# One input's load moved to another queue, and the result stored by one engine: a bilinear form on one core

## The chip, the core and the metric

The kernel runs on one core of one Trainium2 chip. A core has five engines, each with its own queue of instructions: TensorE (PE, the matrix products), VectorE (DVE), ScalarE (ACT), GpSimd (POOL) and SyncE (SP). Data move between the chip's main memory (HBM) and the on-chip memory (SBUF) by sixteen transfer engines, which every engine's DMA instructions feed: the profile calls the queue that GpSimd feeds q0 (software), that of SyncE q1 and that of ScalarE q10 (both hardware). TensorE's results are collected in a separate memory (PSUM) of eight banks.

The metric is the device time of one execution in microseconds. Several executions are timed, and the median counts.

## What is computed

```python
batch, dim_i, dim_j, dim_k = 32, 256, 256, 128
x: [32, 256]   y: [32, 256]   weight: [128, 256, 256]      (all float32)
out = np.einsum('bi,bj,kij->bk', x, y, weight)             # [32, 128]
```

For each of the 128 values of k the weight is a 256 x 256 matrix, and each row b of the result needs x[b] times that matrix times y[b]. The weight has 33.6 MB and is read once; x, y and the result have 32, 32 and 16 KB.

## The kernel before

**Tiling.** k is written as kk * 32 + g, with kk from 0 to 3 and g (a "group") from 0 to 31. The 128 partitions of the weight in SBUF hold four values of kk times 32 slices of i (ip), and each slice has eight values of i (ic). A group is thus a tile of 128 partitions x (8 x 256) values, 1 MB in float32. One product takes the weight of one or two groups at one ic (128 x 256 or 128 x 512) as the moving operand, and as the stationary one xblk[:, ic], a 128 x 128 matrix that holds x in four diagonal blocks, so that the four kk in the partitions stay apart. Eight products, one per ic, add up in PSUM. What comes out, for each group, is a tile of 128 (b, kk) x 256 (j). VectorE multiplies it by y4 (y repeated for each kk) and sums over j, which gives one column of acc [128 x 32].

**Order of the weight.** Thirty of the 32 groups are loaded by GpSimd (L120), which converts them to bfloat16 on the way, in eleven transfers listed in `LOADS`: of 2, 4, 8, 8, 4, 2 and 1 groups, and the last group in four pieces of 4, 2, 1 and 1 values of ic. Groups 0 and 16 (`FIRST`) are loaded as float32 into w_f, one by SyncE and one by ScalarE (L134), and ScalarE converts them (L178). TensorE goes through `UNITS`: 16 groups at once (all eight banks), then 8, 4, 2, 1 and 1. The first unit needs the two groups of `FIRST` and the first three of GpSimd's transfers, each of the later ones its own transfer or transfers. Since the first unit fills all banks, the second waits until VectorE's first product (L294) has freed them.

**The head.** All loads are issued ahead of the barrier with which the engines start (`hw` and `sw`, moved to the head of the program by hand). The queues then hold, in order:

- SyncE: w_f group 0
- ScalarE: x (L130), w_f group 16
- GpSimd: loads 1 and 2 of the weight, y (L127), loads 3 to 11

Behind the barrier GpSimd makes an identity matrix (L168, L169). VectorE's queue holds: the copy of x into x_rep (L192, waits for x), four transposes to xt (L198), the mask from the identity (L205), xblk in four instructions (L210); then y's transpose (L219, waits for y), its copy (L222) and four transposes to y4 (L227); then the products and sums of the units (L294, L298, and L302 for the two units of one group). TensorE's first product waits for w_f's conversion, for xblk and for the loads of its unit (L237).

**The tail.** When VectorE has written the last column of acc, ScalarE stores its partitions 64 to 127 (L311) and SyncE its partitions 0 to 63 (L313). Each then marks a semaphore; GpSimd waits for both marks, and resets the DMA queues' state and the semaphores (L315 to L317). SyncE's last instructions wait until both stores have landed and clear that semaphore (L318, L319).

Of the kernel before, what the change touches and what calls it, by code (L numbers as in the profile page):

```python
# [36 lines left out]
def kernel(  # L37
# [7 lines left out]
    nc = tc.nc  # L45
    P = 128
# [6 lines left out]
    B, I = x.shape  # L53
# [12 lines left out]
    def sbuf(name, shape, dtype):  # L66
        return nc.alloc_sbuf_tensor(name, shape, dtype).ap()

    def rows_of(groups):


        step = G // len(groups)
        assert all(g == groups[0] + n * step for n, g in enumerate(groups))
        v = weight.rearrange("(u s) (ip ic) j -> s ip u (ic j)", s=step, ic=IC)
        return v[groups[0]]

    def w_of(groups):
        at = [place_of[g] for g in groups]
        step = at[1] - at[0] if len(at) > 1 else 1
        assert all(a == at[0] + n * step for n, a in enumerate(at))  # L80
        return w_sb[:, at[0]:at[-1] + 1:step, :]
# [3 lines left out]
    x_sb = sbuf("x_sb", [B, I], f32)  # L85
    y_sb = sbuf("y_sb", [B, J], f32)
# [9 lines left out]
    acc = sbuf("acc", [P, G], f32)  # L96
# [6 lines left out]
        for s, (groups, lo, hi) in zip(s_w, LOADS) for g in groups for ic in range(lo, hi)  # L103
    }
    s_f = [nc.alloc_semaphore(f"f{g}") for g in FIRST]
    s_x = nc.alloc_semaphore("x")
    s_y = nc.alloc_semaphore("y")
# [3 lines left out]
    s_dve = nc.alloc_semaphore("dve")  # L111
    s_fin = nc.alloc_semaphore("fin")
    s_out = nc.alloc_semaphore("out")
# [5 lines left out]
    sw = [  # L119
        nc.gpsimd.dma_start(  # L120
            out=w_of(groups)[:, :, lo * J:hi * J],
            in_=rows_of(groups)[:, :, lo * J:hi * J],
        ).then_inc(s, 16).ins
        for (groups, lo, hi), s in zip(LOADS, s_w)
    ]

    sw.insert(2, nc.gpsimd.dma_start(out=y_sb, in_=y).then_inc(s_y, 16).ins)  # L127

    hw = [
        nc.scalar.dma_start(out=x_sb, in_=x).then_inc(s_x, 16).ins,  # L130
    ]
    for n, (g, queue) in enumerate(zip(FIRST, (nc.sync, nc.scalar))):
        hw.append(
            queue.dma_start(  # L134
                out=w_f[:, n:n + 1, :], in_=rows_of((g,)),
# [13 lines left out]
    for blk in blocks:  # L149
# [15 lines left out]
    pool, act, v, pe, sp = nc.gpsimd, nc.scalar, nc.vector, nc.tensor, nc.sync  # L165
# [4 lines left out]
        out=ident, in_=ident, compare_op=mybir.AluOpType.not_equal, fill=1.0,  # L170
# [13 lines left out]
    n_dve = 0  # L184

    def done(ins):
# [6 lines left out]
        out=x_rep,  # L193
        in_=x_sb.rearrange("b (ip ic) -> b ic ip", ic=IC).unsqueeze(3)
        .to_broadcast([B, IC, IP, KK]),
    )._wait_ge(s_x, 16))
    for q in range(Q):
        c = v.transpose(  # L198
            out=xt[q * 32:(q + 1) * 32, :, :],
            in_=x_rep[:, :, q * IP // Q:(q + 1) * IP // Q, :],  # L200
# [5 lines left out]
        out=mask, in_=ident.rearrange("p (ip kk) -> p kk ip", kk=KK), axis=AX, op=add,  # L206
    )._wait_ge(s_pool, 2))

    for kk in range(KK):
        c = v.tensor_scalar(  # L210
            out=xblk[:, :, :, kk], in0=xt, scalar1=mask[:, kk:kk + 1],
# [8 lines left out]
        out=yt, in_=y_sb.rearrange("b (jb j) -> b jb j", j=32),  # L220
    )._wait_ge(s_y, 16))
    t = done(v.tensor_copy(  # L222
        out=y_rep, in_=yt.unsqueeze(3).to_broadcast([B, J // 32, B, KK]),
    )._wait_ge(s_dve, t))
    BQ = B // Q
    for q in range(Q):
        c = v.transpose(  # L227
            out=y4[q * 32:(q + 1) * 32, :].rearrange("p (jb j) -> p jb j", j=32),
            in_=y_rep[:, :, q * BQ:(q + 1) * BQ, :],
# [22 lines left out]
    for u, unit in enumerate(UNITS):  # L252
# [40 lines left out]
        if n_g > 1:  # L293
            t = done(v.tensor_tensor(  # L294
                out=prod, in0=sums, in1=y4.unsqueeze(1).to_broadcast([P, n_g, J]), op=mult,
# [3 lines left out]
                out=acc[:, unit[0]:unit[-1] + 1:unit[1] - unit[0]], in_=prod, axis=AX, op=add,  # L299
            )._wait_ge(s_dve, t))  # L300
        else:
            done(v.tensor_tensor_reduce(  # L302
                out=prod[:, 0, :], in0=sums[:, 0, :], in1=y4, scale=1.0, scalar=0.0,
# [4 lines left out]


    out_v = out.rearrange("b (kk g) -> b kk g", kk=KK)  # L310
    act.dma_start(out=out_v[B // 2:], in_=acc[P // 2:, :])._wait_ge(s_dve, n_dve).then_inc(s_out, 16)  # L311
    act.sem_inc(s_fin, 1)
    sp.dma_start(out=out_v[:B // 2], in_=acc[:P // 2, :])._wait_ge(s_dve, n_dve).then_inc(s_out, 16)  # L313
    sp.sem_inc(s_fin, 1)
    pool.wait_ge(s_fin, 2)  # L315
    pool.dma_reset(range(nums[0], nums[-1] + 1))
    pool.sem_clear(range(nums[0], nums[-1] + 1))  # L317
    sp.wait_ge(s_out, 32)  # L318
    sp.sem_clear(s_out)  # L319


# [28 lines left out]
```

## Time and profile before

| | |
|---|---|
| time, median of 3 executions | 85.35 us (85.29 to 85.44) |
| profiled execution | 85.44 us, of which the span from the first to the last instruction is 84.1 us |
| busy in the span | PE 33.4 us, DVE 25.0, POOL 8.8, ACT 5.3, PEld 4.3 |
| DMA | 4928 packets; HBM read 33.62 MB |
| queue q0 (GpSimd) | 93.5% of the sixteen engines' span; q1 3.5%, q10 3.4% |
| TensorE's longest wait | 42.0 us, for the loads of w_sb |
| mean granted clock of TensorE | 0.959 |

The profile is that of one execution. PE is TensorE's products, PEld its loading of stationary operands, and an engine's name with a q is its sequencer, which issues DMAs. The strips cut the span into 40 slices of 2.1 us; each digit is a busy share in tenths. GB/s counts the bytes that were written, so a stream that converts float32 to bfloat16 shows half of what it reads. The chain is followed back from the last instruction, at each step to what released it; "another core or an unknown queue" is a releaser that the profile couldn't name, for which the list of waits gives the load. A timeline row gives start, duration, engine, line, operation and, in brackets, how long the engine had been idle and what released it; rows of several instructions give the stretch that they cover. Time to landing is from the start of an issue to the last completion mark.

### The profile page before, as it was taken

Reading aid. Unit: us, or ns where it says so; the run is one execution under the profiler, and the core shown is the slowest. Engines: PE = TensorE matmul, PEld = TensorE weight load, DVE = VectorE, ACT = ScalarE, POOL = GpSimd, SP = SyncE. Lnnn points to the kernel's source line nnn. Section 1 sums busy time; section 2 is a strip of 40 time slices with the busy share of each in tenths; the row PEclk is TensorE's granted clock in tenths of the full one; section 3 lists DMA queues with packets and bytes.
Section 4 is the critical chain, followed back from the end, with each engine's and each line's share of the span. In section 5 each row is a group of like instructions: output and inputs, shape, how many; then the busy total and the mean of one; then the engine's idle time right before and its main releaser. Section 6 shows DMA issues by size and latency. Waiting matters only on the chain.

```text
span 84.1 us, 259 instructions
## 1 busy us (share of the span) xinstructions
PE 33.4 (40%) x136; PEld 4.3 (5%) x43; DVE 25.0 (30%) x28; ACT 5.3 (6%) x5; POOL 8.8 (10%) x18
## 2 busy tenths in 40 slices
PE   0000000000000000000099999997009999997670
PEld 0000000000000000000000000000000010113320
DVE  0019540000291000000000000002999900799950
ACT  0019850000000000000000000000000000000000
POOL 5999500000000000000000000000000000000000
PEclk9999999999999999999999999999855599999999
DMA  4999999999999999999999999999999999999940
GB/s 121 390 362 288 216 216 216 216 214 216 214 216 216 218 216 214 216 210 214 210 218 216 216 216 214 216 216 208 214 214 216 216 216 214 216 208 212 197 59 8
DMA packets 4928, 17.91 MB, mean 213 GB/s; under 512 B 400, under 2 KB 816, under 8 KB 4672
## 3 DMA queue, kind: packets, MB, share of 16 engines
q0 software_dynamic: 4432, 15.76, 93.5%
q1 hardware_dynamic: 224, 1.06, 3.5%
q10 hardware_dynamic: 272, 1.09, 3.4%
HBM read 33.62 MB, written 0.02 MB: 400 GB/s over the span
## 4 chain that ended last, share of the span: by engine, by line
DMA 46%; PE 40%; DVE 6%; POOL 3%; another core or an unknown queue 2%; issue 1%; POOLq 0%
DMA w_sb<-in_weight_dram 46%; PE ps L237 40%; DVE tmp L294 5%; POOL w_sb L120 2%; POOL y_sb L127 1%; DVE tmp L302 1%; POOL const-float32-0.0 L334 0%; POOLq L334 0%; POOL const-uint8-127 L334 0%; POOL const-float32-1.0 L334 0%; DVE acc L302 0%
## 5 line engine op out<-in xcount | busy, mean ns | idle before, releaser
L237 PE MATMUL ps<-w_sb,xblk 128*128 128x512 bf16 (+1 forms) x136 | 33.4, 405 | 48.2 <-DMA w_sb<-in_weight_dram 43.5
L294 DVE TENSOR_TENSOR tmp<-ps,y 128x4096 f32<-128x4096 f32 (+3 forms) x4 | 8.6, 2151 | 37.6 <-PE ps L237 37.6
L298 DVE TENSOR_REDUCE acc<-tmp 128x16 f32<-128x4096 f32 (+3 forms) x4 | 8.6, 2154 | 0.1
L237 PEld LDWEIGHTS ps<-w_sb,xblk 128*128 128x128 bf16 x43 | 4.3, 101 | 77.1 <-DMA w_sb<-in_weight_dram 42.9
L120 POOL DMA_DIRECT2D w_sb<-in_weight_dram x11 | 7.6, 702 | 0.6 <-issue 0.6
L178 ACT CAST w_sb<-w_f 128x1024 bf16<-128x1024 f32 x4 | 4.0, 1042 | 0.3 <-DMA w_f<-in_weight_dram 0.3
L219 DVE STREAM_TRANSPOSE yt<-y_sb 32x256 f32<-32x256 f32 x1 | 0.4, 432 | 11.0 <-DMA y_sb<-in_y_dram 11.0
L192 DVE COPY x_rep<-x_sb 32x1024 f32<-32x1024 f32 x1 | 0.8, 790 | 6.1 <-PEq L334 6.1
L198 DVE STREAM_TRANSPOSE xt<-x_rep 32x256 f32<-32x256 f32 x4 | 1.7, 435 | 0.1
L227 DVE STREAM_TRANSPOSE y<-y_rep 32x256 f32<-32x256 f32 x4 | 1.7, 435 | 0.1
L178 ACT ACT_TABLE_LOAD x1 | 1.3, 1283 | 6.0 <-PEq L334 6.0
L210 DVE TENSOR_SCALAR xblk<-xt,mask 128x256 bf16<-128x256 f32 x4 | 1.4, 501 | 0.0
L302 DVE CUSTOM_DVE_ANT_0 tmp<-ps,y 128x256 f32<-128x256 f32 x2 | 0.8, 419 | 0.9 <-PE ps L237 0.9
L222 DVE COPY y_rep<-yt 32x1024 f32<-32x1024 f32 x1 | 0.7, 682 | 0.0
L205 DVE TENSOR_REDUCE mask<-ident 128x4 f32<-128x128 f32 x1 | 0.4, 380 | 1.0 <-POOL ident L169 1.0
L127 POOL DMA_DIRECT2D y_sb<-in_y_dram x1 | 0.5, 534 | 0.0
L169 POOL TENSOR_SCALAR_AFFINE_SELECT ident<-ident 128x128 f32<-128x128 f32 x1 | 0.3, 287 | 0.1
L168 POOL MEMSET ident<- 128x128 f32 x1 | 0.3, 289 | 0.0
L302 DVE DVE_READ_ACCUMULATOR2_ANT acc<- 128x1 f32 x2 | 0.2, 82 | 0.0
L334 POOL MEMSET const-float32-0.0<- 128x1 f32 x1 | 0.1, 98 | 0.2 <-issue 0.2
L334 POOL MEMSET const-bfloat16-1.0<- 128x1 bf16 x1 | 0.1, 101 | 0.0
L334 POOL MEMSET const-uint8-127<- 128x1 uint8 x1 | 0.1, 101 | 0.0
(1 smaller groups left out, 0.1 us busy)
## 6 DMA issues: line engine op xcount, KB each, us to landing
w_sb<-in_weight_dram POOLq DMA_DIRECT2D x2, 4096.0 KB, 48.1
w_sb<-in_weight_dram POOLq DMA_DIRECT2D x2, 2048.0 KB, 43.4
w_sb<-in_weight_dram POOLq DMA_DIRECT2D x2, 1024.0 KB, 41.0
w_f<-in_weight_dram SPq DMA_DIRECT2D x1, 1024.0 KB, 4.9
w_f<-in_weight_dram ACTq DMA_DIRECT2D x1, 1024.0 KB, 9.0
w_sb<-in_weight_dram POOLq DMA_DIRECT2D x1, 512.0 KB, 72.3
w_sb<-in_weight_dram POOLq DMA_DIRECT2D x1, 256.0 KB, 72.9
w_sb<-in_weight_dram POOLq DMA_DIRECT2D x1, 128.0 KB, 73.0
```

The source lines that it names most:

```text
L120: nc.gpsimd.dma_start(out=w_of(groups)[:, :, lo * J:hi * J], in_=rows_of(groups)[:, :, lo * J:hi * J],).then_inc(s, 16).ins
L127: sw.insert(2, nc.gpsimd.dma_start(out=y_sb, in_=y).then_inc(s_y, 16).ins)
L178: c = act.copy(out=w_sb[:, place_of[g], lo:hi], in_=w_f[:, n, lo:hi])
L192: t = done(v.tensor_copy(out=x_rep, in_=x_sb.rearrange("b (ip ic) -> b ic ip", ic=IC).unsqueeze(3) .to_broadcast([B, IC, IP, KK]),)._wait_ ...
L198: c = v.transpose(out=xt[q * 32:(q + 1) * 32, :, :], in_=x_rep[:, :, q * IP // Q:(q + 1) * IP // Q, :],)
L210: c = v.tensor_scalar(out=xblk[:, :, :, kk], in0=xt, scalar1=mask[:, kk:kk + 1], scalar2=None, op0=mult,)
L222: t = done(v.tensor_copy(out=y_rep, in_=yt.unsqueeze(3).to_broadcast([B, J // 32, B, KK]),)._wait_ge(s_dve, t))
L227: c = v.transpose(out=y4[q * 32:(q + 1) * 32, :].rearrange("p (jb j) -> p jb j", j=32), in_=y_rep[:, :, q * BQ:(q + 1) * BQ, :],)
L237: return pe.add_instruction(mybir.InstMatmult(name=nc.get_next_instruction_name(), engine=mybir.EngineType.PE, ins=[pe.lower_ap(rhs), pe.l ...
L294: t = done(v.tensor_tensor(out=prod, in0=sums, in1=y4.unsqueeze(1).to_broadcast([P, n_g, J]), op=mult,)._wait_ge(s_pe, n_pe))
L298: done(v.tensor_reduce(out=acc[:, unit[0]:unit[-1] + 1:unit[1] - unit[0]], in_=prod, axis=AX, op=add,)._wait_ge(s_dve, t))
L302: done(v.tensor_tensor_reduce(out=prod[:, 0, :], in0=sums[:, 0, :], in1=y4, scale=1.0, scalar=0.0, op0=mult, op1=add, accum_out=acc[:, uni ...
```

## The change

The load of x leaves the head of ScalarE's queue and becomes the third transfer in GpSimd's list, just ahead of y. At the end acc is stored by one transfer of 128 partitions, issued by SyncE, in place of two of 64; ScalarE stores nothing, and the marks that GpSimd and SyncE wait for are halved accordingly.

```diff
-    sw.insert(2, nc.gpsimd.dma_start(out=y_sb, in_=y).then_inc(s_y, 16).ins)
-
-    hw = [
-        nc.scalar.dma_start(out=x_sb, in_=x).then_inc(s_x, 16).ins,
+    sw[2:2] = [
+        nc.gpsimd.dma_start(out=x_sb, in_=x).then_inc(s_x, 16).ins,
+        nc.gpsimd.dma_start(out=y_sb, in_=y).then_inc(s_y, 16).ins,
     ]
+
+    hw = []
     for n, (g, queue) in enumerate(zip(FIRST, (nc.sync, nc.scalar))):
...
     out_v = out.rearrange("b (kk g) -> b kk g", kk=KK)
-    act.dma_start(out=out_v[B // 2:], in_=acc[P // 2:, :])._wait_ge(s_dve, n_dve).then_inc(s_out, 16)
-    act.sem_inc(s_fin, 1)
-    sp.dma_start(out=out_v[:B // 2], in_=acc[:P // 2, :])._wait_ge(s_dve, n_dve).then_inc(s_out, 16)
+    sp.dma_start(out=out_v, in_=acc)._wait_ge(s_dve, n_dve).then_inc(s_out, 16)
     sp.sem_inc(s_fin, 1)
-    pool.wait_ge(s_fin, 2)
+    pool.wait_ge(s_fin, 1)
     pool.dma_reset(range(nums[0], nums[-1] + 1))
     pool.sem_clear(range(nums[0], nums[-1] + 1))
-    sp.wait_ge(s_out, 32)
+    sp.wait_ge(s_out, 16)
     sp.sem_clear(s_out)
```

## The prediction

> **What bounds the kernel now.** I read the page's strips first, then the chain in order of time, then the timeline at the head and at the tail, then the DMA by small windows. The strips show one resource that is never idle between its start and its end:
>
> ```profile
> PE   0000000000000000000099999997009999997670
> ...
> DMA  4999999999999999999999999999999999999940
> GB/s 121 390 362 288 216 216 216 216 214 216 214 216 216 218 216 214 216 210 214 210 218 216 216 216 214 216 216 208 214 214 216 216 216 214 216 208 212 197 59 8
> ...
> HBM read 33.62 MB, written 0.02 MB: 400 GB/s over the span
> ```
>
> The transfer engines are full from the first slice to the 38th (a slice is 2.1 us). The 33.62 MB read between about 1.2 and 80.9 us are 0.42 MB per us. TensorE has half the span free. The chain at its end tells whether TensorE or the stream of weights ends last:
>
> ```profile
> 75.52 0.70 another core or an unknown queue
> ...
> 76.26 1.89 PE ps L237 x8
> 78.15 0.49 another core or an unknown queue
> ...
> 79.72 0.18 another core or an unknown queue
> ...
> 82.03 0.01 DVE acc L302
> ```
>
> Before each of the last small units TensorE waits (0.70, 0.49, 0.18 us); the waits' own view names the landing of w_sb. So the end follows the stream: whatever shifts its last packets shifts the last reduction by as much, and a delay of TensorE up to 0.7 us is swallowed. Behind the reduction stands only the store, both halves issued at 82.07, until the span closes at 84.1. Two places can therefore move the time: the length of the stream, and the 2.0 us of the store.
>
> **The change, part by part.** The profiled execution took 85.44 us: a span of 84.10 and 1.34 around it. It is the highest of the three (median 85.35); the terms are made against it and then laid on the median.
>
> ```profile
> 0.00 0.66 SPq L134 DMA_DIRECT2D w_f<-in_weight_dram  x1
> 0.12 0.43 ACTq L130 DMA_DIRECT2D x_sb<-in_x_dram  x1
> 0.59 0.62 ACTq L134 DMA_DIRECT2D w_f<-in_weight_dram  x1
> ...
> 2.65 0.53 POOL L127 DMA_DIRECT2D y_sb<-in_y_dram  x1
> 3.18 5.96 POOL L120 DMA_DIRECT2D w_sb<-in_weight_dram  x9
> ...
> 22.58 0.43 DVE L219 STREAM_TRANSPOSE yt<-y_sb 32x256 f32<-32x256 f32 x1 [11.04 <-DMA y_sb<-in_y_dram]
> ...
> 42.04 16.27 PE L237 MATMUL ps<-w_sb,xblk 128*128 128x512 bf16 x64 [42.04 <-DMA w_sb<-in_weight_dram]
> ```
>
> *x comes late, and it is hidden.* On GpSimd's queue x stands behind the same two loads as y, so it lands where y lands, near 22.5 us. VectorE's first instruction waits for x, and in its queue the mask, xblk and the whole of y's preparation stand behind it. From 22.5: the copy 0.79, four transposes 1.83, mask 0.38, xblk 1.37, together 4.4 us, so xblk is there at 27. Then y's own 0.43 + 0.68 + 1.83 = 2.9, so y4 is there at 30. TensorE's first product needs xblk and starts at 42.04 because of the third load; VectorE's first use of y4 is at 58.35. Cover 15 and 28 us: cost nothing. Without the cover each us would cost a us less the 0.7 of slack.
>
> *GpSimd issues one transfer more,* 0.53 us by y's row. The nine loads behind it go out 0.53 later, the first at 3.71 instead of 3.18; its turn on the transfer engines comes after y, near 22. Covered by 18 us. The identity matrix (9.07) and the start barrier, which waits for GpSimd and frees the other engines at about 6.0, move as much; the casts of w_f then end near 12.1 instead of 11.6, needed at 42.04. Nothing.
>
> *ScalarE loses x's issue* (0.43), so its w_f load is issued at about 0.12 instead of 0.59. That transfer is served after SyncE's w_f (landed at 4.9) and its data are not needed before 42: no gain of its own.
>
> *The stream gets x inside it.* Its 32 KB now stand in the saturated stretch: 0.033 MB / 0.42 = 0.08 us. The trace's packet records show y doing just this at 21.5 us: one packet per engine and a completion mark, 0.096 us until the next load's packets. I take +0.09, with 0.08 and 0.10 as ends.
>
> *The stream's start gets rid of x.* The windows at the head, then the two small waves of the store's halves (columns at the end: granted clock, DMA share, GB/s):
>
> ```profile
> 1.00:1.20 0.20, 0.00 (x0) 0.00 (x0) 0.00 (x0) 0.00 (x0) 0.15 (x1) 1.00 0.08 31
> 1.20:1.50 0.30, 0.00 (x0) 0.00 (x0) 0.00 (x0) 0.00 (x0) 0.30 (x1) 1.00 0.98 198
> 1.50:1.80 0.30, 0.00 (x0) 0.00 (x0) 0.00 (x0) 0.00 (x0) 0.30 (x1) 1.00 1.31 328
> ...
> 83.20:83.30 0.10, 0.00 (x0) 0.00 (x0) 0.00 (x0) 0.00 (x0) 0.00 (x0) 1.00 0.20 32
> ...
> 83.50:83.60 0.10, 0.00 (x0) 0.00 (x0) 0.00 (x0) 0.00 (x0) 0.00 (x0) 1.00 0.31 46
> ```
>
> By the packet records x runs from 1.17 to 1.53; w_f's first packets come at 1.43 to 1.71 on the sixteen engines, 1.54 in the mean. If x only held the engines up, w_f may start at its issue's end plus what x needed after its own: 0.66 + 0.63 = 1.29, a gain of 0.25 at most. If w_f's 128 rows simply take 1.43 us from issue to first packet, only the late engines gain, 0.05 to 0.1. It can also lose: the two w_f issues now stand side by side as the two halves of the store do, and there the one whose issue started 5 ns later got its packets 0.27 us after the other (83.24 and 83.51). SyncE's stays the first by 0.12 us, so I take -0.05, with -0.25 and +0.27 as ends.
>
> *The store in one piece.* SyncE's half landed 1.7 us after its issue, ScalarE's 2.0, and SyncE's wait for both ended the span.
>
> ```profile
> out_dram<-acc SPq DMA_DIRECT2D x1, 8.0 KB, 1.7
> out_dram<-acc ACTq DMA_DIRECT2D x1, 8.0 KB, 2.0
> ```
>
> No row shows a store of 128 rows. The times from the start of an issue to the first packet are 1.05 us for 32 rows (x), 1.18 for 64 (SyncE's half), 1.43 for 128 (w_f): 4 ns per row. So the single store's first packet would come at 82.07 + 1.43 = 83.50, just where the later half's came (83.51). Then each engine has eight packets instead of four, about 12 ns each by the records: +0.05. Ends: as quick as SyncE's half, 2.0 - 1.7 = -0.30; or the second half's packets spread out behind the first's for another 0.27 us on top of today's end, +0.27. I take +0.05, since three rows lie on one line. GpSimd's clean-up waits for one engine's mark instead of two; in the records it ends near 83.0, a microsecond before the span: nothing.
>
> A rule speaks to this part. The Trainium skill, page "DMA: Bandwidth & Descriptors", section "Rules for kernel authors", says that two transfers to disjoint partition halves serialize and that one 128-partition transfer is to be used; by it the merge costs nothing, the term would be 0 and the time 85.39. The two waves in the windows agree that the halves follow each other. The same page, "Latency and other measured facts", gives a first byte about 0.4 us later for a transfer issued from GpSimd than from ScalarE, which speaks against moving x; by it x would be late by 0.4 us, against the 20 us that the trace's y row shows.
>
> Sum: +0.09 - 0.05 + 0.05 = +0.09. On the profiled execution 85.53, on the median **85.44 us**.
>
> **The rivals.** A difference below 0.2% (0.17 us) can hardly be told from none here; the forecast lies below that.
>
> 1. *The store in one piece is the slower one.* Place: the last 2 us, where nothing overlaps. For it: x's 32 rows, two packets per engine, spread over 0.36 us, and w_f's first packets over 0.28, where a half of the store took 0.2. Price: +0.27 with +0.04 of the stream, 85.66. It decides once the store lands later than 2.13 us after its issue (0.13 + 0.04 = 0.17). Against it: the line of the three rows.
> 2. *The head of the stream is held up* by two 128-row issues side by side: +0.27 + 0.09 + 0.05, 85.76. For it: ScalarE's half of the store. Against it: x's issue lay inside that of w_f and delayed it by little or nothing.
> 3. *The store is as quick as SyncE's half:* -0.30 + 0.04, 85.09. It decides from a landing under 1.79 us. For it: one completion to wait for, and the wave of a half is gone. Against: twice the rows for one queue.
> 4. *x is late for TensorE.* It needs xblk after 42.0, so x after 37.6; y says 22.5. Should x's issue stall behind the third load (landing near 41), xblk would come near 46, and the end 4 - 0.7 = 3.3 us later, 88.7. Against: the order of the queue.
>
> **How the numbers follow.** Forecast (within 0.2%) 0.47; rival 1 0.21; rival 2 0.15; rival 3 0.15; rival 4 0.02. Slower is 0.21 + 0.15 + 0.02 = 0.38, faster 0.15. The range reaches from just above rival 3's price to rival 2's, 85.17 to 85.78: it leaves out most of rival 3, rival 4, and the far end of rival 2, some 2 in 10. The forecast's own range is 85.18 to 85.52.
>
> **What would show it.** In the profile after: x_rep starts near 22.6 and the first product near 42.1; the waits of TensorE before the last units are as long as before; the last products come 0.04 us later; one out store whose landing stands between 1.9 and 2.1. Wrong would be: a first product moved by over 0.2 us, a landing outside that, or a first window of the stream that starts later.

## The result, and the profile after

The changed kernel takes 85.02 us (median of 6 executions, 84.97 to 85.10), the kernel before, timed beside it, 85.39 us (85.29 to 85.49). The ratio is 0.9957, with a 95% interval of 0.9944 to 0.9969: faster by 0.37 us, or 0.43%. The forecast was no change that can be told, 85.44 us, and the range began at 85.17: the measured time lies below all of it.

The profiled execution took 84.97 us, with a span of 83.6; before it was 85.44 and 84.1. So the difference of the two profiles is 0.47 us and lies inside the span. The strips of the page of the changed kernel:

```profile
span 83.6 us, 257 instructions
...
PE   0000000000000000000089999999205999999780
...
DMA  3999999999999999999999999999999999999970
GB/s 67 415 345 317 221 214 217 214 206 219 225 214 216 219 216 217 217 214 206 216 219 216 217 217 206 214 216 219 216 216 216 208 216 216 217 216 217 194 110 8
...
HBM read 33.62 MB, written 0.02 MB: 402 GB/s over the span
```

The picture is the same: the transfer engines are full up to the 38th slice. The timeline of the changed kernel at the steps that the prediction named (start, duration, engine, line, operation):

```profile
0.00 0.63 SPq L135 DMA_DIRECT2D w_f<-in_weight_dram  x1
0.12 0.60 ACTq L135 DMA_DIRECT2D w_f<-in_weight_dram  x1
...
2.64 0.53 POOL L128 DMA_DIRECT2D x_sb<-in_x_dram  x1
3.17 0.52 POOL L129 DMA_DIRECT2D y_sb<-in_y_dram  x1
...
22.62 0.68 DVE L193 COPY x_rep<-x_sb 32x1024 f32<-32x1024 f32 x1 [22.62 <-DMA x_sb<-in_x_dram]
...
27.96 1.83 DVE L228 STREAM_TRANSPOSE y<-y_rep 32x256 f32<-32x256 f32 x4
...
42.13 16.88 PE L238 MATMUL ps<-w_sb,xblk 128*128 128x512 bf16 x64 [42.13 <-DMA w_sb<-in_weight_dram]
...
82.16 0.35 SPq L312 DMA_DIRECT2D out_dram<-acc  x1
```

x arrives at 22.6, y4 is ready at 29.8, TensorE still starts when the third load lands, at 42.13 instead of 42.04. The store is issued at 82.16 instead of 82.07: up to there the changed kernel is 0.09 us *behind*. From the issue it then needs 1.45 us to SyncE's last instruction, which waits for the store to land and stands 0.03 us before the end of the span; the kernel before needed 2.00. This is how all the stores below are measured. The whole gain is in that stretch. The issue itself is shorter, 0.35 us for 128 partitions where each half of 64 took 0.52 and 0.55, and the landing comes earlier. The rows of DMA issues (KB, us from issue to landing) and the windows of the store (the last columns are granted clock, DMA share, GB/s):

```profile
out_dram<-acc SPq DMA_DIRECT2D x1, 16.0 KB, 1.4
...
82.90:83.00 0.10, 0.00 (x0) 0.00 (x0) 0.00 (x0) 0.00 (x0) 0.00 (x0) 1.00 0.01 1
83.00:83.10 0.10, 0.00 (x0) 0.00 (x0) 0.00 (x0) 0.00 (x0) 0.00 (x0) 1.00 0.59 95
83.10:83.20 0.10, 0.00 (x0) 0.00 (x0) 0.00 (x0) 0.00 (x0) 0.00 (x0) 1.00 0.47 66
83.20:83.30 0.10, 0.00 (x0) 0.00 (x0) 0.00 (x0) 0.00 (x0) 0.00 (x0) 1.00 0.02 3
```

One wave from 83.0 to 83.2 stands where two stood, at 83.2 and 83.5. In the packet records (the trace's list of what each transfer engine moved, packet by packet) its first packet comes 0.84 us after the start of the issue; the halves' came 1.18 and 1.44 after theirs.

### The profile page after: what moved, and what is told of

Read it like the earlier page. It is cut to its first block, busy times and chain, and to the rows that moved or that the text cites. A ratio compares the mean times of both kernels' runs of the same rounds, so it can differ in the third digit from the quotient of the medians.

```text
span 83.6 us, 257 instructions
## 1 busy us (share of the span) xinstructions
PE 34.1 (41%) x136; PEld 4.3 (5%) x43; DVE 24.6 (29%) x28; ACT 5.2 (6%) x5; POOL 9.3 (11%) x19
## 4 chain that ended last, share of the span: by engine, by line
DMA 46%; PE 32%; DVE 16%; POOL 3%; issue 1%; POOLq 0%
DMA w_sb<-in_weight_dram 46%; PE ps L238 32%; DVE tmp L295 10%; DVE acc L299 5%; POOL w_sb L120 2%; DVE tmp L303 1%; POOL x_sb L128 1%; POOL y_sb L129 1%; POOL const-float32-0.0 L333 0%; POOLq L333 0%; POOL const-uint8-127 L333 0%; POOL const-float32-1.0 L333 0%; DVE acc L303 0%
## 5 line engine op out<-in xcount | busy, mean ns | idle before, releaser
L238 PE MATMUL ps<-w_sb,xblk 128*128 128x512 bf16 (+1 forms) x136 | 34.1, 413 | 47.6 <-DMA w_sb<-in_weight_dram 42.8
L193 DVE COPY x_rep<-x_sb 32x1024 f32<-32x1024 f32 x1 | 0.7, 681 | 22.6 <-DMA x_sb<-in_x_dram 22.6
L128 POOL DMA_DIRECT2D x_sb<-in_x_dram x1 | 0.5, 534 | 0.0
```

The lines of the kernel that those rows point to most:

```text
L128: nc.gpsimd.dma_start(out=x_sb, in_=x).then_inc(s_x, 16).ins,
L193: t = done(v.tensor_copy(out=x_rep, in_=x_sb.rearrange("b (ip ic) -> b ic ip", ic=IC).unsqueeze(3) .to_broadcast([B, IC, IP, KK]),)._wait_ ...
L238: return pe.add_instruction(mybir.InstMatmult(name=nc.get_next_instruction_name(), engine=mybir.EngineType.PE, ins=[pe.lower_ap(rhs), pe.l ...
```

## The experiments

The theories, by the letters that the expectations use. A: two issues at once, from two queues, slow each other. B, and later N: a second transfer costs, whatever queue it is in. C: the gain comes from x leaving ScalarE's head. D: ScalarE's queue is the slow one. P came up after the first four runs, from a difference in the built programs: the builder marks some DMA instructions for a form of issue that is prepared when the program is built. The store of all 128 partitions carries that mark, and so does x's load at ScalarE's head; neither half of 64 partitions does, nor do the loads of w_f, whose source has three dimensions. P says that this form is what gained. The marks are read in the built programs, which aren't printed here; the issue times of hardware queues fit them: 0.34 to 0.43 us for transfers read as marked (x's load, whole stores, halves by columns), 0.49 to 0.67 for those read as unmarked. Why the builder marks a store of 128 partitions and not one of 64 isn't known.

All times are medians, with the ratio to the kernel before, timed beside it, and its 95% interval. Gains and losses in us are worked out from the ratios; where two runs are compared, the interval is that of the difference of their ratios. Everything read from a profile is one execution.

### The two parts apart

The change of x alone:

```diff
+    sw[2:2] = [
+        nc.gpsimd.dma_start(out=x_sb, in_=x).then_inc(s_x, 16).ins,
+        nc.gpsimd.dma_start(out=y_sb, in_=y).then_inc(s_y, 16).ins,
+    ]
+    hw = []
...
     act.dma_start(out=out_v[B // 2:], in_=acc[P // 2:, :])._wait_ge(s_dve, n_dve).then_inc(s_out, 16)
```

> x third on GpSimd's queue as in the change; the store stays in two halves as before. Theory A (the gain is the store's: two issues at once, one by SyncE and one by ScalarE, slow each other): slower than before by 0.05 to 0.10 us, 85.45 beside 85.37; from the store's issue to the end of the span 2.0 us as before; the stream's last packet about 0.05 later, at 81.01. Theory C (the gain comes from x leaving the head of ScalarE's queue): faster than before by 0.3 to 0.4 us.

Measured: 85.53 us, ratio 1.0016 (1.0005 to 1.0027); slower by 0.14 us, somewhat more than A's 0.05 to 0.10. The store is issued at 82.16, as in the changed kernel, and takes as long as before (rows below).

The store alone, with x left at ScalarE's head:

```diff
+    sp.dma_start(out=out_v, in_=acc)._wait_ge(s_dve, n_dve).then_inc(s_out, 16)
```

> x stays at the head of ScalarE's queue; one store of 128 partitions by SyncE. Theory A: faster than before by 0.4 to 0.55 us, 84.85 to 84.95; the issue lasts 0.35 us instead of 0.52 and the store's landing is 1.4 us instead of 2.0. Theory C: no more than 0.1 us faster than before.

Measured: 84.85 us, ratio 0.9933 (0.9919 to 0.9948); faster by 0.57 us, and faster than the changed kernel too. The store with x alone moved, then with the store alone changed:

```profile
82.16 0.52 SPq L314 DMA_DIRECT2D out_dram<-acc  x1
82.16 0.53 ACTq L312 DMA_DIRECT2D out_dram<-acc  x1
...
out_dram<-acc SPq DMA_DIRECT2D x1, 8.0 KB, 1.7
out_dram<-acc ACTq DMA_DIRECT2D x1, 8.0 KB, 2.0
```

```profile
81.98 0.34 SPq L311 DMA_DIRECT2D out_dram<-acc  x1
...
out_dram<-acc SPq DMA_DIRECT2D x1, 16.0 KB, 1.4
```

C falls. The two parts pull against each other: the store gains 0.57, x loses 0.14, and the sum, 0.43, is the changed kernel's 0.37 within the intervals. From its issue the single store takes 1.44 us, the halves 2.01.

### Which engine, and one queue instead of two

The one store by ScalarE:

```diff
-    sp.dma_start(out=out_v, in_=acc)._wait_ge(s_dve, n_dve).then_inc(s_out, 16)
-    sp.sem_inc(s_fin, 1)
+    act.dma_start(out=out_v, in_=acc)._wait_ge(s_dve, n_dve).then_inc(s_out, 16)
+    act.sem_inc(s_fin, 1)
```

> The changed kernel with the one store issued by ScalarE instead of SyncE. Theory A: the same as the changed kernel within 0.1 us, an issue of 0.35 us and a landing at 1.4 to 1.5 us. A rival D, that ScalarE's queue is the slow one (its half landed at 2.0 where SyncE's landed at 1.7): a landing at 1.7 or more, and 0.25 us slower than the changed kernel.

Measured: 84.98 us, ratio 0.9952 (0.9938 to 0.9967), an issue of 0.35 us and a landing at 1.4. D falls: for this store the queue makes no difference.

The halves of 64 partitions again, both by SyncE, in the changed kernel:

```diff
+    sp.dma_start(out=out_v[:B // 2], in_=acc[:P // 2, :])._wait_ge(s_dve, n_dve).then_inc(s_out, 16)
+    sp.dma_start(out=out_v[B // 2:], in_=acc[P // 2:, :]).then_inc(s_out, 16)
...
```

> The changed kernel, but its store is again in two halves, both issued by SyncE, one after the other. Theory A (two queues issuing at the same time is what costs): each issue lasts 0.3 us or less, the second half lands 1.7 us after the first issue's start, 0.15 to 0.3 us later than the one store; the time is 85.15 to 85.3, between the two kernels. Theory B (a second transfer costs, whatever queue it is in): like the kernel before, 2.0 us from the first issue to the end, 85.4.

Measured: 85.99 us, ratio 1.0071 (1.0051 to 1.0092). Its two issues, and their landing, in the timeline and the list of issues:

```profile
82.20 0.49 SPq L312 DMA_DIRECT2D out_dram<-acc  x1
82.74 0.59 SPq L313 DMA_DIRECT2D out_dram<-acc  x1
...
out_dram<-acc SPq DMA_DIRECT2D x2, 8.0 KB, 1.7
```

Neither theory forecast this. The first half is issued while nothing else is, and still takes 0.49 us; by the packet records its first packet comes 1.15 us after the start, as in the kernel before. A said 0.3 or less. So the half is slow by itself, and A can't be the whole of the gain. Two queues even help the halves: in one queue the second starts 0.55 later, and the end comes 2.35 us after the first issue instead of 2.0.

### The form of the issue, and the number of transfers

The same single store as in the changed kernel, without the mark:

```diff
+    nc.dge_precook = False
     sp.dma_start(out=out_v, in_=acc)._wait_ge(s_dve, n_dve).then_inc(s_out, 16)
```

> The changed kernel, the same one store of 128 partitions by SyncE, but built with the builder's mark for the prepared form of issue switched off for this store (in the changed kernel the store of the whole tile carries that mark; in the kernel before neither half did). Theory P (the gain is the prepared form's): the issue lasts 0.5 to 0.6 us instead of 0.35, the first packets come 1.15 to 1.4 us after its start instead of 0.84, and the time goes back to 85.35 to 85.6. Theory N (the gain is that there is one transfer and one completion instead of two): nothing changes, 85.0.

Measured: 85.33 us, ratio 0.9983 (0.9971 to 0.9995). Beside the changed kernel's 0.9957 that is 0.22 us back.

```profile
82.31 0.54 SPq L313 DMA_DIRECT2D out_dram<-acc  x1
...
out_dram<-acc SPq DMA_DIRECT2D x1, 16.0 KB, 1.8
```

The issue takes 0.54 instead of 0.35, the first packet comes 1.19 us after its start instead of 0.84, and the end 1.79 instead of 1.45. The bytes, rows, queue and waits are the same, so these 0.34 us are the form's in the two profiles. By the times it is 0.22, with an interval of 0.07 to 0.37. But the store is still ahead of the halves' 2.0, and its time 0.28 us (0.14 to 0.42) ahead of the halves with x moved, so P alone doesn't make up the gain.

Two transfers that both carry the mark, cut by columns:

```diff
+    out_2 = out.rearrange("b (kk g) -> (b kk) g", kk=KK)
+    act.dma_start(out=out_2[:, G // 2:], in_=acc[:, G // 2:])._wait_ge(s_dve, n_dve).then_inc(s_out, 16)
+    act.sem_inc(s_fin, 1)
+    sp.dma_start(out=out_2[:, :G // 2], in_=acc[:, :G // 2])._wait_ge(s_dve, n_dve).then_inc(s_out, 16)
...
```

> The changed kernel, its store again in two transfers, one by SyncE and one by ScalarE at the same moment, but cut by columns: 128 partitions x 16 columns each, which do carry the mark. Theory P: both issues last about 0.35 us, the later of them lands 1.4 to 1.65 us after its start, and the time is 85.0 to 85.2. Theory N: as slow as the kernel before, 2.0 us from issue to end, 85.4.

Measured: 85.12 us, ratio 0.9959 (0.9946 to 0.9972). Then the same without the mark:

```diff
+    nc.dge_precook = False
     out_2 = out.rearrange("b (kk g) -> (b kk) g", kk=KK)
```

> The store in two halves by columns, by SyncE and ScalarE at the same moment, as before, but with the mark for the prepared form switched off for both. Theory P with a second term (form 0.34 us, second transfer 0.2 us, and they add): 1.98 us from the issue to the end of the span instead of 1.64, and a time of 85.4 to 85.55, that of the kernel before with x moved. If the form counted only for a store that stands alone: 1.65 us, and 85.15.

Measured: 85.64 us, ratio 1.0028 (1.0015 to 1.0040). The stores of the first and of the second kernel:

```profile
82.17 0.35 SPq L315 DMA_DIRECT2D out_dram<-acc  x1
82.17 0.36 ACTq L313 DMA_DIRECT2D out_dram<-acc  x1
...
out_dram<-acc SPq DMA_DIRECT2D x1, 8.0 KB, 1.5
out_dram<-acc ACTq DMA_DIRECT2D x1, 8.0 KB, 1.6
```

```profile
82.19 0.54 SPq L316 DMA_DIRECT2D out_dram<-acc  x1
82.19 0.54 ACTq L314 DMA_DIRECT2D out_dram<-acc  x1
...
out_dram<-acc SPq DMA_DIRECT2D x1, 8.0 KB, 1.8
out_dram<-acc ACTq DMA_DIRECT2D x1, 8.0 KB, 2.0
```

Two issues at the same moment last as long as one (0.35 and 0.36; 0.54 and 0.54), so A falls for the issue itself. The packets are another matter: without the mark those of ScalarE's queue come 0.27 us behind SyncE's (83.65 and 83.38, the same distance as in the kernel before), with it 0.04 (83.05 and 83.01). That much of A stands, for unmarked transfers. From the start of the first issue to SyncE's last instruction, in us:

| store | with the mark | without |
|---|---|---|
| one transfer, 128 partitions | 1.45 | 1.79 |
| two, 128 partitions x 16 columns | 1.64 | 2.05 |
| two, 64 partitions x 32 columns | not marked by the builder | 2.01 |

In these profiles the form is worth 0.34 to 0.41 us, a second transfer costs 0.19 to 0.26, and the way from the lower right corner to the upper left one is 0.56. Each entry is one execution, and the times split the same sum otherwise:

| in the times | us | interval |
|---|---|---|
| the form, one transfer | 0.22 | 0.07 to 0.37 |
| the form, two by columns | 0.59 | 0.43 to 0.74 |
| a second transfer, with the mark | 0.02 | -0.14 to 0.17 |
| a second transfer, without | 0.38 | 0.24 to 0.53 |

So both parts are there, and either way leads to some 0.6, but how they share it is known only roughly; that a second transfer costs anything where both are marked isn't shown. Halves by columns also have 64-byte packets, and twice as many, where the others have 128 bytes; that part isn't taken apart. What the form saves in the issue of the single store (0.19) is a bit over half of its 0.34; the rest comes between the end of the issue and the first packet (0.65 without, 0.49 with).

### The head of the stream

Both loads of w_f by SyncE, in the changed kernel:

```diff
-    for n, (g, queue) in enumerate(zip(FIRST, (nc.sync, nc.scalar))):
+    for n, (g, queue) in enumerate(zip(FIRST, (nc.sync, nc.sync))):
```

> The changed kernel with both loads of w_f issued by SyncE, one behind the other, ScalarE none. Theory A (two issues at once slow each other): the first issue lasts 0.4 us instead of 0.63, w_f's first packets come at 0.9 to 1.1 us instead of 1.40, and the time falls by 0.2 to 0.4 us to 84.6 to 84.8. Theory P (what counts is the form of the issue; these loads carry no mark in either kernel): the first issue lasts 0.6 us and the first packets come at 1.4 as now; the time is that of the changed kernel within 0.1 us.

Measured: 84.88 us, ratio 0.9935 (0.9916 to 0.9954). The two issues take 1.27 us together, the first 0.63 as before, and in the packet records w_f's first packet comes at 1.44. That is P's forecast for the head and not A's. Yet the time is just above A's range and below P's, 0.19 us under the changed kernel with intervals that overlap: the last packet of the stream leaves at 80.83 instead of 81.01. Most of the difference is there from the start: the completion marks of GpSimd's first load (each of the sixteen transfer engines sends one behind its share of a load) come at 11.85 us in the mean, instead of 11.98. Why is open.

One store, x and y both at ScalarE's head:

```diff
     hw = [
         nc.scalar.dma_start(out=x_sb, in_=x).then_inc(s_x, 16).ins,
+        nc.scalar.dma_start(out=y_sb, in_=y).then_inc(s_y, 16).ins,
     ]
```

> The one store of the changed kernel, with x at the head of ScalarE's queue as before, and y behind it there too instead of in GpSimd's list. With x back at the head the time was 84.85, 0.17 below the changed kernel. If a small load costs 0.1 to 0.15 us inside the saturated stream and nothing ahead of it, y's move gains that again: 84.70 to 84.78. If instead the packets of x and y hold up the first packets of w_f, nothing is gained: 84.85 to 84.95.

Measured: 86.11 us, ratio 1.0080 (1.0050 to 1.0111). The stream has 32 KB less in it than with x alone at the head, and ends later. Its windows at the end (the last two columns are DMA share and GB/s), then its chain there:

```profile
80.80:81.00 0.20, 0.12 (x2) 0.00 (x0) 0.04 (x1) 0.00 (x0) 0.00 (x0) 1.00 0.39 51
81.00:81.20 0.20, 0.06 (x1) 0.05 (x1) 0.20 (x1) 0.00 (x0) 0.00 (x0) 1.00 0.14 20
81.40:81.60 0.20, 0.20 (x4) 0.06 (x1) 0.00 (x0) 0.00 (x0) 0.00 (x0) 1.00 0.08 10
82.00:82.20 0.20, 0.20 (x3) 0.06 (x1) 0.00 (x0) 0.00 (x0) 0.00 (x0) 1.00 0.06 8
```

```profile
76.19 1.20 another core or an unknown queue
...
79.32 0.53 another core or an unknown queue
```

For more than a microsecond a share of 0.06 to 0.14 is busy: one or two of sixteen transfer engines (one is 0.0625). The packet records of the completion marks say since when. Those of GpSimd's first load come between 12.14 and 12.63 on fifteen engines and at 13.60 on one. A last mark a microsecond behind the others is still there 58 us later (71.22 and 72.18 for the load of groups 3, 11, 19 and 27); the records don't name the engine, so that it is the same one is inferred. In the kernel before the last engine marks the first load 0.14 us after the last but one (12.31 and 12.17). Packets of y, issued at 0.58, start only at 4.00, when the last of SyncE's w_f (at 4.64) are near. Neither case of the expectation came: instead of no gain there is a loss of 1.26 us beside the store alone changed, which nobody forecast. About a microsecond of it is the one engine, behind since the first load, with which the stream ends; the others end 0.3 to 0.4 us later too. What throws the engine back isn't shown.

x alone at ScalarE's head, both loads of w_f by SyncE, one store:

```diff
         nc.scalar.dma_start(out=x_sb, in_=x).then_inc(s_x, 16).ins,
...
+    for n, (g, queue) in enumerate(zip(FIRST, (nc.sync, nc.sync))):
```

> One store of 128 partitions by SyncE; x alone at the head of ScalarE's queue; both loads of w_f issued by SyncE. x out of the stream was worth 0.17 us (84.85 beside 85.02), both w_f loads in one queue about 0.15 to 0.2 (84.88). If the two add up: 84.65 to 84.75. If both only even out the same lag of the last transfer engine: 84.8 to 84.9. If x's packets beside w_f's throw one engine back, as y's did: above 85.

Measured: 84.87 us, ratio 0.9937 (0.9922 to 0.9953). The gains don't add. The time is that of the expectation's second case, but its reason isn't shown: the last packet leaves at 81.04, where with x in the stream and the same w_f loads it left at 80.83. So moving x out of the stream is not always a gain: with w_f's loads in one queue the time stays the same (0.02 us apart), and the first load's marks come at 12.07 in the mean instead of 11.85, so what is saved in the stream is lost at its head. What each order of the first transfers does there was not settled. The fastest kernel of all runs is the one with the store alone changed, 84.85 us; those with both w_f loads by SyncE are as fast within their intervals.

## Why the prediction was wrong, by its steps

**What bounds the kernel: right.** The stream of weights runs unbroken in every run, and only its length and the store moved the time. One thing was put too simply: that the end follows the stream because TensorE waits before the last units, and that these waits would stay. In the profile after, the chain's last nine microseconds are VectorE's:

```profile
73.11 2.30 DVE tmp L295
...
75.43 2.29 DVE acc L299
77.72 1.14 DVE tmp L295
...
81.76 0.36 DVE tmp L303
82.12 0.01 DVE acc L303
```

The second unit's product ends there a microsecond later (73.1 instead of 72.1), after which VectorE has no gap. The first unit took 16.88 us of TensorE instead of 16.27, and the half-clock stretch (see the end) lay at 61.7 to 68.5 instead of 60.4 to 67.2. It cost nothing that can be told: VectorE begins the last column at 81.70, TensorE's last product ends at 81.66. But the slack was used up. Nor is it shown to come from the change: the profile with x alone moved has a wait of 1.25 us before the same unit, and the one with the store alone changed has VectorE's chain, though the store comes behind it.

**x comes late, and it is hidden: right,** with the numbers (22.6; y4 at 29.8 instead of 30; 42.13). The Trainium skill's 0.4 us between the two ways of issuing ("DMA: Bandwidth & Descriptors", "Latency and other measured facts") can't be seen here: x lands 20 us after its issue, because of its place in the queue.

**GpSimd's extra issue, ScalarE's lost one: right.** The barrier moves from 6.0 to 6.5 and nothing follows.

**The stream: right in sign, too small.** The forecast was +0.09 for x inside and -0.05 for its leaving the start, +0.04 together. Measured: the last packet leaves at 81.01 to 81.16 in the seven profiles with x third in GpSimd's queue and the w_f loads by two engines (mean 81.05), and at 80.96 and 80.87 in the two with x at ScalarE's head (mean 80.91): +0.14; the time of that part alone is +0.14 too (0.04 to 0.23). The -0.05 is what did not come: w_f's first packets start at 1.51 us in the mean of the sixteen engines instead of 1.55, but between 1.51 and 1.78 in the seven profiles as in the two, so there is no earlier start to speak of. The completion marks tell the two apart. In the mean the seven profiles are 0.06 later than the two at GpSimd's first and second loads, both ahead of x, and 0.14 later at the third, behind it, and it stays so. So x inside costs its 0.09, and the head loses 0.06 where the prediction had it gain 0.05: the direction of rival 2, at a quarter of its price. One thing differs there: SyncE's w_f doesn't land at 4.9 any more, ahead of ScalarE's, but at 5.8. That this is the cause isn't shown, and with w_f's loads in one queue the sign turns, as said above.

**The store in one piece: this step failed.** The prediction put it at +0.05; it is -0.56 in the profiles, and -0.57 in the time of the kernel with the store alone changed. The working took the time to the first packet from a line through three transfers and read a price per row out of it. The three differ in more than their rows: x's load carries the mark for the prepared form, the other two don't; x's rows have 1 KB and w_f's 8 KB, and both are read from HBM. Without the mark a store of 128 partitions needs 1.19 us to its first packet, hardly more than one of 64 with its 1.18: there is no price per row to speak of. With the mark it is 0.84, where the prediction had 1.43. So the step failed twice: the form of the issue was not in the sum at all (0.34 us in the profiles, 0.22 in the times), and the missing second transfer was given nothing (0.22 in the profiles, 0.28 in the times). The lower end of the term, -0.30, came from SyncE's half landing at 1.7; a store that is *faster* than the smaller one was left out, although nothing in the profile excluded it.

The Trainium skill's rule, one 128-partition transfer rather than two halves ("DMA: Bandwidth & Descriptors", "Rules for kernel authors"), points the right way here; the prediction took it as neutral. Without the mark the single store is 0.28 us ahead of the two partition halves in the times, and their packets follow each other in two waves.

**The rivals.** The third, a store as quick as SyncE's half, had the right place and sign and 0.15 of the chance; its price of -0.30 was half of what came. The first, a store that is slower in one piece, didn't occur. The second, a head held up by two issues side by side, came to 0.06 us instead of 0.27; the issues themselves were no longer than one alone (0.63 and 0.60). The fourth was never near.

## What to carry to other kernels

A price read off the issue of one transfer holds for another only if both have the same form, and a line through transfers of different kinds proves nothing. Where a store stands alone at the end, write it as one transfer over all 128 partitions, and look in the built program whether the builder has marked it; in this kernel that was worth 0.57 us. A small load inside a saturated stream costs about 0.1 us, but moving it to the head isn't sure to save that: here it saved 0.2 us, or nothing, or lost 1.3, depending on what else stood there. Look at the completion marks of all transfer engines after such a move: the slowest one ends the stream.

## What the runs showed of the hardware that wasn't expected

- The larger store was issued faster: 0.34 to 0.35 us for 128 partitions, 0.49 to 0.59 for 64, in whichever queue, and whether or not another was issued beside it. Switching off the builder's mark alone made it 0.54, and the first packet came 1.19 us after the start of the issue instead of 0.84.
- Two stores issued at the same moment by two queues sent their packets 0.27 us apart without the mark, and 0.04 apart with it.
- A lag from the head of the stream wasn't made up. In the kernel with x and y at ScalarE's head the last engine's mark lagged by 0.97 us at 13.6 us and by as much at 72 us, and the stream ended 1.2 us later although it carried less.
- The stretch in which TensorE's granted clock is halved differs between executions of nearly the same work: 6.83 us from 60.4 in the kernel before, 6.83 from 61.7 in the changed one, and 3.41 from 63.1 with x alone moved. Windows of 61.70 to 68.50 in the changed kernel and of 63.11 to 66.52 with x alone moved show it (the granted clock is the third number from the end):

```profile
61.70:68.50 6.80, 4.91 (x12) 0.44 (x3) 6.20 (x2) 0.00 (x0) 0.00 (x0) 0.50 1.08 218
...
63.11:66.52 3.41, 3.41 (x10) 0.30 (x2) 3.41 (x1) 0.00 (x0) 0.00 (x0) 0.50 1.05 213
```
